# Reading the moving operand, and writing the sums, from the last token to the first

## The chip, the cores and the metric

The kernel runs on one core of a Trainium2 chip. The metric is the device time of one execution in microseconds, as the median of several runs. All times below are of this one core.

## What is computed

A two-layer decoder trunk over 256 tokens of width 1024, with a memory of 256 rows. Cut to what matters:

```python
def reference(x, mem, positions, ...):
    h = x
    for layer in range(2):
        hn = rmsnorm(h, norm_mix_g[layer])
        h = h + (sb_moba_mixer if layer == 0 else fox_mixer)(hn, ...)     # q/k/v (and gate) projections, 16 heads, output projection
        h = h + memory_cross_attention(rmsnorm(h, norm_xa_g[layer]), rmsnorm(mem, norm_mem_g[layer]), ...)
        h = h + conv_ffn(rmsnorm(h, norm_ffn_g[layer]), ...)              # up 1024 -> 2 x 2816, causal conv of width 3, silu(gate) * val, down
    return rmsnorm(h, final_norm_g)
```

Most of the arithmetic lies in products of weights with activations: the projections of the mixers, those of the cross-attention and the two of the MLP.

## The kernel before

Activations are held transposed: 128 features on the partitions, 256 tokens along the row, eight such tiles for the width of 1024. A product therefore has the weights as the stationary operand (128 x 128) and a tile of tokens as the moving one (128 x 256), and its sums lie in PSUM as 128 features by 256 tokens.

Precision is kept by splitting. Each weight block comes in as f32 (`raw`, loaded by SP's queue), ScalarE rounds it to the reduced type float32r (`whi`, line 126) and VectorE subtracts to get the rest (`wlo`, line 127). Activations are split likewise into a high and a low tile. A product of the two is then three products on TensorE: high by high, weight-high by activation-low, weight-low by activation-high. `proj` (lines 262 to 272) writes them, all on line 268, and every product on that line loads its own 128 x 128 weights. For a width of 1024 that makes 24 products into one PSUM tile; the down-projection has 66, in three weight blocks.

The names in the profile are those of the tiles. Moving tiles of line 268: `xh`/`xl` (the normed residual; 8 pairs), `gh`/`gl` (head outputs, the normed memory, and the MLP's gated values; 16 pairs), `part` (the first six of the MLP's gated pairs), `xn` (the renormalised input of the up-projection, 8 pairs from line 755 on). Sums: `acc` (two PSUM banks) and `sc` (four). The pools `xin`, `qkv` and `parts` that hold the moving tiles, and `wsp` that holds `whi` and `wlo`, lie in SBUF with gaps of 64, 256 and 64 bytes set by `shift`.

`proj_nat` (line 282) is the other form of product, with the activations as the stationary operand and the weights moving; it makes the values of the attentions and isn't touched. Attention scores, transposes (line 414, 697, 840), rope's product with a constant rotation (line 474, in f32), and the sums of squares for the norms (line 241, one moving column) aren't touched either.

The order on TensorE is the order in which the code is written (a manual schedule for that engine); the other engines are ordered by the tile scheduler. In the mixers attention steps are interleaved with the projections by `Pipe`; in the MLP of each layer 44 up-projections of 24 products follow one another, then 8 down-projections of 66.

The consumers of the sums read a whole PSUM tile once its last product is done: `evac_row` and `residual` (line 519) on VectorE, `glu` on ScalarE and VectorE, in ascending order of tokens.

Of the kernel before, what the change touches and what calls it, by code (L numbers as in the profile page):

```python
# [69 lines left out]
def trunk(ctx: ExitStack, tc: tile.TileContext, a: dict, out: bass.AP):  # L70
    nc = tc.nc
# [72 lines left out]
    for k in range(KD // 2):  # L144
        s = slice(k * 2 * P, (k + 1) * 2 * P)
# [116 lines left out]
    def proj(b, off, xs, ps, first=True, last=True, m=P, hooks={}):  # L262
        n = 0
        for k, (xh, xl) in enumerate(xs):
            s = slice(off + k * m, off + k * m + m)
            end = last and k == len(xs) - 1
            for w, x in ((b.hi, xh), (b.hi, xl), (b.lo, xh)):
                nc.tensor.matmul(ps[:m], w[:, s], x, start=first and n == 0, stop=end and w is b.lo)  # L268
                n += 1
                if n in hooks:  # L270
                    hooks[n]()
        return ps
# [268 lines left out]
    def mixer(layer, st):  # L541
# [47 lines left out]
        for g in range(4):  # L589
            def pair(i, hooks=({}, {})):  # L590
                wi = w[6 * g + 4 * i:6 * g + 4 * i + 2]
                q = proj(block(wi[0]), 0, xs, accA(), hooks=hooks[0])
                if hooks[0]:
                    return q, lambda: proj(block(wi[1]), 0, xs, accA(), hooks=hooks[1])
                q = evac_row(q, st, "q", 3, True)
                pipe.tick()
                k = evac_row(proj(block(wi[1]), 0, xs, accA()), st, "k", 3, False)
                pipe.tick()
                return q, k
# [344 lines left out]
```

## Time and profile before

| | |
|---|---|
| median of 3 runs | 716.21 us (714.2 to 717.5) |
| profiled execution | 717.27 us |
| its span, first to last instruction | 715.5 us |
| mean granted TensorE clock | 0.991 |
| TensorE busy | 695.3 us (97%), 5,751 products |
| weight loads busy (overlap TensorE) | 666.2 us (93%), 5,751 |
| VectorE, ScalarE, GpSimd busy | 575.1, 467.6, 74.2 us |
| HBM read | 114.25 MB, 161 GB/s over the span |

Engines in the rows: PE is TensorE's products, PEld its weight loads, DVE is VectorE, ACT ScalarE, POOL GpSimd. A row of a group gives line, engine, operation, output<-inputs by tile name, shape, count, busy time in us and the mean of one in ns. The time of one product in the rows (some 0.28 us) is from its start to the modelled end of its sums; products overlap, so the pace is read from start to start. In a row that merges several instructions, the time runs from the first's start to the last's end.

### The profile page before, as it was taken

How to read it: one execution, taken by the hardware profiler on the slowest of the kernel's cores; microseconds unless marked ns; L12 is line 12 of the kernel's file. 1: busy time of each engine (PE TensorE's matmuls, PEld its weight loads, DVE VectorE, ACT ScalarE, POOL GpSimd, SP SyncE). 2: the span in 40 equal slices, each digit the busy share in tenths (PEclk: the TensorE clock that was granted, in tenths of full speed). 3: DMA queues.
4: the chain of work that ended last, by engine and by line, in shares of the span. 5: the costliest groups of instructions: out<-in, count | busy, mean ns of one | idle time of the engine just before them, and what ended most of it. 6: DMA issues, size and time to landing. Idle time of an engine off the chain costs nothing. (4 is left out here: it accounts for less than half of the span.)

```text
span 715.5 us, 15077 instructions
## 1 busy us (share of the span) xinstructions
PE 695.3 (97%) x5751; PEld 666.2 (93%) x5751; DVE 575.1 (80%) x1195; ACT 467.6 (65%) x942; POOL 74.2 (10%) x82
## 2 busy tenths in 40 slices
PE   8989999999999999999999999999999999999995
PEld 5979998988999999999999889898899999999995
DVE  6997698687999988856669989958889998886541
ACT  6876866577787766644466868746778776664431
POOL 1200020212400000001200000012150000000110
PEclk9989999999999999999999999999999999999998
DMA  8745432343565655565651743515346566656601
GB/s 299 284 145 180 148 119 89 93 148 113 207 189 196 209 195 175 170 186 167 214 164 33 265 125 112 177 56 182 119 177 178 196 210 193 186 164 189 184 6 59
DMA packets 34968, 116.32 MB, mean 163 GB/s; under 512 B 4080, under 2 KB 6224, under 8 KB 34896
## 3 DMA queue, kind: packets, MB, share of 16 engines
q1 hardware_dynamic: 34896, 115.36, 50.8%
q8 instruction: 45, 0.74, 0.4%
q14 instruction: 27, 0.22, 0.1%
HBM read 114.25 MB, written 1.05 MB: 161 GB/s over the span
## 5 line engine op out<-in xcount | busy, mean ns | idle before, releaser
L126 ACT ACTIVATE whi<-raw 128x512 fp32r<-128x512 f32 (+2 forms) x296 | 231.0, 807 | 129.3 <-PE acc L268 80.8
L127 DVE TENSOR_TENSOR wlo<-raw,whi 128x512 fp32r<-128x512 f32 (+2 forms) x296 | 269.1, 925 | 56.4 <-ACT whi L126 54.1
L268 PE MATMUL sc<-xn,whi 128*128 128x256 f32 x768 | 136.9, 281 | 0.0
L268 PEld LDWEIGHTS sc<-xn,whi 128*128 128x128 f32 x768 | 117.9, 189 | 0.0
L268 PE MATMUL acc<-gh,whi 128*128 128x256 f32 x400 | 113.3, 283 | 0.2
L268 PE MATMUL acc<-gl,whi 128*128 128x256 f32 x400 | 111.5, 279 | 0.1
L268 PE MATMUL acc<-gh,wlo 128*128 128x256 f32 x400 | 111.2, 278 | 0.0
L268 PE MATMUL sc<-xn,wlo 128*128 128x256 f32 x384 | 107.9, 281 | 0.0
L268 PE MATMUL acc<-xh,whi 128*128 128x256 f32 x336 | 98.6, 293 | 2.4 <-DVE h L519 0.9
L268 PE MATMUL acc<-xh,wlo 128*128 128x256 f32 x336 | 94.4, 281 | 2.5 <-DVE wlo L127 2.5
L268 PE MATMUL acc<-xl,whi 128*128 128x256 f32 x336 | 95.4, 284 | 0.7 <-DVE xl L175 0.6
L226 POOL TENSOR_TENSOR sq<-sq 128x256 f32<-128x256 f32 x42 | 41.3, 984 | 508.6 <-ACT sq L220 467.6
L268 PEld LDWEIGHTS acc<-gh,whi 128*128 128x128 f32 x400 | 75.5, 189 | 2.3 <-ACT gh L170 0.9
L268 PEld LDWEIGHTS acc<-gl,whi 128*128 128x128 f32 x400 | 75.1, 188 | 0.3 <-DVE gl L171 0.3
L268 PEld LDWEIGHTS acc<-gh,wlo 128*128 128x128 f32 x400 | 75.4, 188 | 0.0
L268 PEld LDWEIGHTS sc<-xn,wlo 128*128 128x128 f32 x384 | 72.9, 190 | 0.0
L268 PEld LDWEIGHTS acc<-xh,whi 128*128 128x128 f32 x336 | 64.0, 190 | 7.0 <-issue 2.5
L268 PE MATMUL acc<-xn,whi 128*128 128x256 f32 x384 | 68.9, 281 | 0.0
L268 PEld LDWEIGHTS acc<-xh,wlo 128*128 128x128 f32 x336 | 63.8, 190 | 2.9 <-DVE wlo L127 2.9
L268 PEld LDWEIGHTS acc<-xl,whi 128*128 128x128 f32 x336 | 63.8, 190 | 2.5 <-DVE xl L175 1.9
L268 PEld LDWEIGHTS acc<-xn,whi 128*128 128x128 f32 x384 | 58.9, 189 | 0.0
L268 PE MATMUL acc<-xn,wlo 128*128 128x256 f32 x192 | 54.0, 281 | 0.0
(218 smaller groups left out, 1402.5 us busy)
## 6 DMA issues: line engine op xcount, KB each, us to landing
raw<-up SPq DMA_DIRECT2D x88, 512.0 KB
raw<-down SPq DMA_DIRECT2D x32, 448.0 KB
raw<-fox_in SPq DMA_DIRECT2D x24, 512.0 KB
raw<-ab_in SPq DMA_DIRECT2D x23, 512.0 KB
raw<-down SPq DMA_DIRECT2D x16, 512.0 KB
raw<-ab_out SPq DMA_DIRECT2D x8, 512.0 KB
raw<-fox_out SPq DMA_DIRECT2D x8, 512.0 KB
raw<-xa_k SPq DMA_DIRECT2D x4, 512.0 KB
```

Source lines behind the costliest of these rows:

```text
L126: i = nc.scalar.activation(hi[:, s], raw[:, s], AF.Copy)
L127: j = nc.vector.tensor_sub(lo[:, s], raw[:, s], hi[:, s].bitcast(F32))
L226: nc.gpsimd.tensor_tensor(sq, sq, self.acc, op=ALU.add)
L268: nc.tensor.matmul(ps[:m], w[:, s], x, start=first and n == 0, stop=end and w is b.lo)
```

## The change

On line 268 both the moving operand and the output get a reversed free axis. The weights stay as they are. The instruction then carries a step of -1 element and the address of the last column as its start, for the moving tile and for the PSUM tile alike, so column j of the moving tile still gives column j of the sums. This holds for all 4,632 products of `proj`, the 16-row forget-gate product among them. The order of instructions on every engine is the same as before, and so are all SBUF and PSUM addresses of tiles.

```diff
             for w, x in ((b.hi, xh), (b.hi, xl), (b.lo, xh)):
-                nc.tensor.matmul(ps[:m], w[:, s], x, start=first and n == 0, stop=end and w is b.lo)
+                nc.tensor.matmul(ps[:m][:, ::-1], w[:, s], x[:, ::-1], start=first and n == 0, stop=end and w is b.lo)
                 n += 1
```

## Prediction

> **What bounds the kernel now.** I read the page first: the share of each engine, the clock, the chain that ended last. The rows are the page's.
>
> ```profile
> span 715.5 us, 15077 instructions
> ...
> PE 695.3 (97%) x5751; PEld 666.2 (93%) x5751; DVE 575.1 (80%) x1195; ACT 467.6 (65%) x942; POOL 74.2 (10%) x82
> ...
> PEclk9989999999999999999999999999999999999998
> ...
> PE acc L268 14%; PE sc L268 11%; PE acc L282 0%; POOL sq L226 0%; DVE wlo L127 0%; DVE mx L685 0%; PE sc L697 0%; ACT sq L220 0%; PE sc L840 0%; PE misc L256 0%; DVE part L313 0%; DVE xl L175 0%; PE po L732 0%; ACT xh L174 0%; DVE h L519 0%
> ```
>
> TensorE is busy for 97% of the span at nearly the full clock, and the chain that ended last is almost wholly line 268, the line that the change edits. Next, the stretches view: line 268 alone over the whole span (TensorE busy, and the count in brackets), then four stages with all engines.
>
> ```profile
> 0.00:715.50 715.50, 562.17 (x4632) 0.99 0.51 163
> ```
>
> ```profile
> core 0: us, PE busy (x) PEld busy (x) DVE busy (x) ACT busy (x) POOL busy (x), PEclk, DMA share, GB/s
> ...
> 200.00:300.00 100.00, 100.00 (x851) 100.00 (x851) 92.86 (x162) 69.31 (x116) 0.00 (x0) 1.00 0.60 191
> 300.00:360.00 60.00, 60.00 (x522) 60.00 (x522) 36.83 (x47) 28.44 (x43) 7.68 (x7) 1.00 0.63 185
> ...
> 540.00:640.00 100.00, 100.00 (x852) 100.00 (x851) 93.40 (x163) 70.51 (x117) 0.00 (x0) 1.00 0.61 191
> 640.00:700.00 60.00, 60.00 (x517) 60.00 (x516) 33.37 (x45) 24.85 (x33) 6.48 (x6) 1.00 0.42 122
> ```
>
> 4,632 products are edited. In the four MLP stretches TensorE never rests, and the pace is 320 us / (851 + 522 + 852 + 517) = 116.7 ns a product. So the question of this change is one number: the time from one product's start to the next's. Every nanosecond of it is worth 4.6 us over the kernel, less what the waits between stages give back. TensorE's largest wait on another engine is small, so little can be given back:
>
> ```profile
> PE acc L268 <- DVE wlo L127: 2.5, 2, 1.8
> ```
>
> What sets the pace? In the timeline of TensorE (start, then time in us, products merged per row) I take three stretches that differ in the moving tile.
>
> ```profile
> 364.74 0.28 PE L268 MATMUL acc<-xl,whi 128*128 128x256 f32 x1
> ...
> 365.87 0.28 PE L268 MATMUL acc<-xh,wlo 128*128 128x256 f32 x1
> ```
>
> ```profile
> 254.82 0.28 PE L268 MATMUL acc<-xn,wlo 128*128 128x256 f32 x1
> ...
> 256.00 0.40 PE L268 MATMUL sc<-xn,whi 128*128 128x256 f32 x2
> ```
>
> ```profile
> 300.77 0.28 PE L268 MATMUL acc<-part,wlo 128*128 128x256 f32 x1
> ...
> 301.61 0.40 PE L268 MATMUL acc<-part,whi 128*128 128x256 f32 x2
> ```
>
> Between the first and last row lie 10, 10 and 7 starts: 1.13 / 10 = 113 ns, 1.18 / 10 = 118 ns, 0.84 / 7 = 120 ns. Same shape, same line, same clock, three paces. They aren't tied to a tile for good, as the chain shows in layer 1's down-projection (66 products in 7.80 and in 7.65 us, so 118.2 and 115.9 ns) and in its up-projection (48 in 5.65 us, 117.7 ns):
>
> ```profile
> 530.50 5.65 PE sc L268 x48
> ...
> 654.25 7.80 PE acc L268 x66
> ...
> 662.27 7.65 PE acc L268 x66
> ```
>
> The weight loads sit beside the products. The first two rows are loads in the 113 ns stretch; the third, at the kernel's end, is loads for products that stream a single column.
>
> ```profile
> 364.86 0.19 PEld L268 LDWEIGHTS acc<-xh,whi 128*128 128x128 f32 x1
> 364.97 0.19 PEld L268 LDWEIGHTS acc<-xl,whi 128*128 128x128 f32 x1
> ...
> ```
>
> ```profile
> 707.88 0.74 PEld L241 LDWEIGHTS misc<-const,sq 128*128 128x128 f32 x6 [0.99 <-ACT sq L220]
> ```
>
> Six loads in 0.74 us, one of them 0.19 long: (0.74 - 0.19) / 5 = 110 ns each, though there is next to nothing to stream. So loading 128 weight columns costs 110 ns by itself, and each product of line 268 needs a fresh load: the loop of load and start is a floor near 113 ns whatever the 256 moving columns do, and those columns must fit in it already, since 113 ns is reached.
>
> **The change part by part.** Nothing is added, removed or moved: the same 4,632 instructions in the same order, with the same weights and waits. Two address patterns of each run backwards, the moving tile's 256 columns in SBUF and the 256 sums in PSUM. Both are turned alike, so every sum lands where it did, and all 24 (or 42, or 66) products of one accumulation go the same way. Whoever reads a PSUM tile waits for the last product of it as before, and each product's 256 columns are complete at the same moment; no reader can start earlier or later for the direction. SBUF traffic, DMA and the other engines are untouched. So the sum has one term, 4,632 times the change of the pace, and no row of this trace shows a backward pattern on TensorE. I bound it.
>
> From below: the pace can't fall under the load's loop, 113 ns. All 4,632 from 116.7 to 113 would be 17 us less. The likelier partial gain is that the products on xn, which run at 117.7 to 118 now, drop to 113. Their counts:
>
> ```profile
> L268 PE MATMUL sc<-xn,whi 128*128 128x256 f32 x768 | 136.9, 281 | 0.0
> L268 PE MATMUL sc<-xn,wlo 128*128 128x256 f32 x384 | 107.9, 281 | 0.0
> L268 PE MATMUL acc<-xn,whi 128*128 128x256 f32 x384 | 68.9, 281 | 0.0
> ...
> L268 PE MATMUL acc<-xn,wlo 128*128 128x256 f32 x192 | 54.0, 281 | 0.0
> ```
>
> That is 1,728 x 4.7 = 8 us. VectorE would still follow: it is busy 92.86 of 100 us there, and that stage would shrink to 113 / 117.7 x 100 = 96 us.
>
> From above there are two bounds. If backward reads keep every address clash and add some, the nearest row is the part tiles' 120 ns: 4,632 x 3.3 = 15 us more. And if TensorE can't take two neighbouring columns together when they descend, the nearest row is an f32 product of the same width, rope's line 474, which issues one product on q and one on k; each shows as two records:
>
> ```profile
> 87.70 0.59 PE L474 MATMUL misc<-q,const 128*128 128x256 f32 x2
> 88.14 0.59 PE L474 MATMUL misc<-k,const 128*128 128x256 f32 x2
> ```
>
> 0.44 us for two records, 220 ns each, against 117 ns: a pass of 256 columns at about half the rate. That would be 4,632 x 103 = 477 us more.
>
> I take zero. The stream has to fit under a 110 ns load, so a start-up cost of a few nanoseconds is covered by the load, and a descending walk touches the same addresses as an ascending one, neighbour after neighbour. That cover is gone as soon as the stream itself takes longer than the load's loop; then all of the excess is paid, because TensorE has no idle time.
>
> The Trainium skill speaks to the paces: TensorE: Matmul & The Clock Gate, section "Step-by-step: what each phase is for", says that the moving operand and the weight load have a read port of SBUF each, so that loading the next weights takes nothing from the running product. By that rule the direction of one stream could not matter to the other, and the sum would be zero with no gain or loss of the 113-to-120 kind. The trace doesn't bear it out fully: 113, 118 and 120 ns at one shape and one clock say that operands' places or the two streams' phase matter.
>
> **The rivals.** Forecast A, the pace stays as it is, stage by stage: 717.3 us for the profiled execution, 1.1 us above the median of the three runs, so 716 as the median, 712 to 720 with the spread of the runs (714.2 to 717.5).
>
> B, faster: running the other way, the moving reads meet the weight reads at other moments, and more of the kernel runs at 113 ns. For it: the three paces above, with 118 held through the whole of both up-projections. Against it: one and the same tile kind (the down-projection's) shows 118.2 and 115.9 ns in alternate column blocks, so the pace also hangs on how a stretch began, and that the change leaves alone. From 716 - 17 = 699 to about 712; the xn products alone give 708.
>
> C, slightly slower: the same mechanism with the other sign. All at 118 is 4,632 x 1.3 = 6 us more, 722; all at 120 is 731. For it: nothing held the reversed phase at 113, and only a part of the kernel is at 113 now, which can be lost. Against it: the floor and the ceiling are both near, so most of the kernel can only lose 2 ns.
>
> D, much slower: descending columns are taken one at a time, by SBUF's reads or by PSUM's writes, and the stream replaces the load as the bound. It decides as soon as the stream passes some 113 ns a product. 716 + 477 = 1,193 us, with TensorE busy throughout and all other engines waiting for it. For it: line 474 shows that this array does walk 256 columns at 220 ns in one mode, so the full rate isn't given for every kind of operand. Against it: neighbours stay neighbours; only their order turns.
>
> The Trainium skill has a rule that would bring D about. Advanced Engine Details and Errata, section "PSUM Cachelines", says "Any non-contiguous AP significantly slows down matmuls". It goes on that every two consecutive elements should be contiguous, in lines of 8 bytes, that is two f32 sums; columns 255 and 254 share such a line, and by that sentence nothing would be lost. No run shown here has a backward or stepped PSUM write of TensorE, so the trace decides neither reading.
>
> That the change doesn't do what it says is A again: if the turned patterns were brought back into ascending order on the way to the chip, the time is 716.
>
> **How the numbers follow.** A 0.37, B 0.26, C 0.20, D 0.17. A is the likeliest, so 716. The range leaves out D, far off and with 0.17 of the chance, and spans B to C: 699 to 731, rounded in to 700 and out to 732; A's own is 712 to 720. Half a per cent, about what a measurement of this kernel can tell from no change, is 3.6 us. A spills 0.02 to each side; B counts as faster (0.28 in all), C and D as slower (0.39), which leaves 0.33.
>
> **What would show it.** In the profile after, one figure decides: the starts of line 268's products in the timeline of the same stretches. A: 118 ns on xn, 120 on part, 113 or 118 on xh and gh, and 48 of them in 5.65 us in the chain. B: 113 on xn, and the up-projection's 48 in 5.4 us. C: the 113 ns stretches gone, or paces over 118. D: some 215 to 220 ns everywhere, PEld's rows with gaps of 0.1 us, VectorE's share of the span near 50% instead of 80%. If only one of the two patterns costs something, the profile after can't say which; a kernel with one of them turned would. The forecast is wrong if line 268's mean pace in the 200 to 300 us stretch moves by over 1 ns.

## The result and the profile after

| | before | after |
|---|---|---|
| median of 8 runs each | 715.21 us (710.04 to 719.13) | 721.82 us (718.89 to 723.39) |
| ratio, 95% interval | | 1.0113 (1.0077 to 1.0149) |
| span of the profiled execution | 715.5 us | 721.6 us |
| mean granted clock in it | 0.991 | 0.986 |

The change costs 1.1%, which is rival C of the prediction and not the forecast. The page after, the same three lines:

```profile
span 721.6 us, 15078 instructions
...
PE 702.9 (97%) x5751; PEld 673.9 (93%) x5751; DVE 575.2 (80%) x1195; ACT 467.8 (65%) x942; POOL 73.9 (10%) x82
...
PEclk7989999999999999999999999999999999999999
```

TensorE is busy for the same share and the other engines for the same time, so no engine has become a new bound. In the stretches view, the four MLP stages (columns as before):

```profile
200.00:300.00 100.00, 100.00 (x851) 100.00 (x851) 93.30 (x163) 70.41 (x117) 0.00 (x0) 1.00 0.61 191
300.00:360.00 60.00, 60.00 (x509) 60.00 (x509) 37.17 (x48) 29.11 (x44) 6.66 (x6) 1.00 0.61 182
...
540.00:640.00 100.00, 100.00 (x851) 100.00 (x850) 93.99 (x163) 71.62 (x119) 1.95 (x3) 1.00 0.59 187
640.00:700.00 60.00, 60.00 (x511) 60.00 (x510) 36.23 (x50) 27.14 (x38) 6.39 (x5) 1.00 0.47 137
```

The up-projections, on xn, are as they were: 851 and 851 products in 100 us against 851 and 852. The stretches of the down-projections are slower: 509 products in 60 us against 522 (117.9 ns against 114.9), and 511 against 517 (117.4 against 116.1). TensorE's timeline shows which pace has gone. In this place before, on the gh tiles, nine starts took 1.02 us, 113 ns each:

```profile
310.64 0.28 PE L268 MATMUL acc<-gh,whi 128*128 128x256 f32 x1
...
311.66 0.28 PE L268 MATMUL acc<-gh,whi 128*128 128x256 f32 x1
```

After, nine starts on the gh tiles take 1.06 us, 118 ns each:

```profile
309.74 0.28 PE L268 MATMUL acc<-gh,whi 128*128 128x256 f32 x1
...
310.80 0.28 PE L268 MATMUL acc<-gh,whi 128*128 128x256 f32 x1
```

The chain says the same of layer 1, whose column blocks took 7.80 and 7.65 us in turn and now take 7.81 each:

```profile
535.95 5.65 PE sc L268 x48
...
659.90 7.81 PE acc L268 x66
667.92 7.81 PE acc L268 x66
```

Counted over all products of line 268 that follow one another within 135 ns (4,472 before, 4,458 after), the mean from start to start is 116.7 ns before and 118.0 after. Before, 1,232 of them came after 113 or 114 ns; after, one did. The products come in the same order in both, so each of these times can be set beside its own in the other profile. The fast ones of before take 5.6 us more in sum, all the others together 0.04 us more: within the pace, the loss is the fast pace and nothing else.

The spans differ by 6.1 us, and that this is so near 5.6 us is partly chance. The first 20 us hold 20 products fewer after than before, which put the changed kernel 2.5 us behind; the granted clock in them was 0.74 in place of 1.00 (before, then after):

```profile
0.00:20.00 20.00, 16.86 (x86) 12.24 (x87) 12.69 (x31) 11.67 (x25) 3.07 (x8) 1.00 0.87 310
```

```profile
0.00:20.00 20.00, 16.73 (x66) 12.00 (x67) 10.81 (x24) 11.53 (x23) 2.23 (x8) 0.74 0.86 310
```

In the rest, shorter gaps on line 268 and on the other lines gave back 2.0 us, nearly all of it in the mixers and the cross-attentions.

### The profile page after: what moved, and what is told of

It reads as the page before. It is cut to its first block, busy times and chain, and to the rows that moved or that the text cites. A ratio compares the mean times of both kernels' runs of the same rounds, so it can differ in the third digit from the quotient of the medians.

```text
span 721.6 us, 15078 instructions
## 1 busy us (share of the span) xinstructions
PE 702.9 (97%) x5751; PEld 673.9 (93%) x5751; DVE 575.2 (80%) x1195; ACT 467.8 (65%) x942; POOL 73.9 (10%) x82
## 5 line engine op out<-in xcount | busy, mean ns | idle before, releaser
L268 PE MATMUL acc<-gh,wlo 128*128 128x256 f32 x400 | 112.7, 282 | 0.0
L268 PE MATMUL acc<-xh,whi 128*128 128x256 f32 x336 | 100.2, 298 | 2.5 <-ACT xh L174 1.5
L268 PE MATMUL acc<-xh,wlo 128*128 128x256 f32 x336 | 96.2, 286 | 2.0 <-DVE wlo L127 2.0
L268 PE MATMUL acc<-xl,whi 128*128 128x256 f32 x336 | 97.2, 289 | 0.4
```

The source lines that it names most:

```text
L268: nc.tensor.matmul(ps[:m][:, ::-1], w[:, s], x[:, ::-1], start=first and n == 0, stop=end and w is b.lo)
```

## Experiments: which of the two patterns

**Only the reads reversed.**

```diff
-                nc.tensor.matmul(ps[:m][:, ::-1], w[:, s], x[:, ::-1], ...
+                nc.tensor.matmul(ps[:m], w[:, s], x[:, ::-1], ...
```

> Only the moving operand is reversed; the sums are written first token to last, so their tokens come out in reverse order and the output is not the reference's. Reading theory (the slowdown comes from the order in which the moving columns are fetched from SBUF while the next weights are fetched): as the changed kernel, ratio to before 1.008 to 1.015, no stretch at 113 ns a product, and a period of three in the up-projection near 120, 115, 118 ns. Writing rival (descending PSUM writes cost the time): as before, within 0.4% of it, with 113 ns stretches in the first mixer and 117 to 118 ns in the up-projection. Chance rival (which of two paces a stretch falls into is a matter of how it began, and the profiled runs only differed in that): both paces again in some mixture, ratio 0.995 to 1.01.

Measured: 721.05 us, ratio 1.007 (1.0041 to 1.0099), just under the expected 1.008. In its stretches view and its chain:

```profile
300.00:360.00 60.00, 60.00 (x509) 1.00 0.59 183
...
640.00:700.00 60.00, 60.00 (x511) 1.00 0.44 132
```

```profile
657.77 7.81 PE acc L268 x66
```

The counts, 509 and 511, and the 7.81 us are those of the changed kernel; in the up-projection the starts go 120, 115, 118 ns round and round, as they do there.

**Only the writes reversed.**

```diff
-                nc.tensor.matmul(ps[:m][:, ::-1], w[:, s], x[:, ::-1], ...
+                nc.tensor.matmul(ps[:m][:, ::-1], w[:, s], x, ...
```

> Only the output is reversed; the moving operand is read first token to last, so the tokens of the sums come out in reverse order and the output is not the reference's. Reading theory: as before, ratio 0.996 to 1.004, 113 ns stretches there. Writing rival: as the changed kernel, ratio 1.008 to 1.015, no 113 ns stretch, period of three near 120, 115, 118 ns. Chance rival: both paces in some mixture, ratio 0.995 to 1.01.

Measured: 718.25 us, ratio 1.0008 (0.9967 to 1.0050).

```profile
300.00:360.00 60.00, 60.00 (x521) 1.00 0.60 185
```

```profile
656.11 7.80 PE acc L268 x66
664.13 7.65 PE acc L268 x66
```

521 products and the turns of 7.80 and 7.65 us: the kernel before. So the reads carry the loss and the writes carry nothing that can be measured. The reading theory held in both, by the traces more clearly than by the times: 1,568 starts came after 113 or 114 ns with the writes reversed, none with the reads reversed. That 1,568 is more than the 1,232 of the kernel before, which suggests that the share of the fast pace changes from one execution to the next; with one trace of each kernel this is not shown.

## Experiments: the pace by itself

**A bench of line 268's products alone.** The rest of the kernel is left out; the loop, run twice for a group of 48 products, is

```python
for k in range(8):
    ...
    for wi, xi in ((0, 0), (0, 1), (1, 0)):      # hi*hi, hi*lo, lo*hi
        m = x[xi][:, off + k * T:off + (k + 1) * T]
        nc.tensor.matmul(acc[:, ::-1] if write else acc, w[wi][:, s], m[:, ::-1] if read else m, ...)
```

> Leaves out the whole network: 64 groups of 48 products in the same pattern (weight-high by high, weight-high by low, weight-low by high), each with its own weight load, with nothing else running, at eight distances in SBUF between moving tile and weights (64 bytes apart, letters A to H), each in four ways: both ascending (up), both descending (down), only the reads descending (read), only the writes descending (write), and all that twice with two lengths of pause ahead of a group. Reading theory: write equals up and read equals down at every distance, within 0.5 ns a product; up shows 113 ns at some distances or some of its groups, down and read never below 117. Writing rival: read equals up, and write equals down. Chance rival: 113 and 118 ns come up in all four ways, without regard to direction. If the distance sets the pace, up differs between letters by up to 7 ns (113 to 120) and repeats between its two passes; if only the beginning sets it, the two passes differ.

Distance is the moving tile's address in SBUF less that of the weights, modulo 256 bytes. In its chain each group is a row: start, time of 48 products, the way and the letter. Letters A to D stand for 0, 64, 128 and 192 bytes; E to H, 256 bytes on, repeat them. From a group's first start to its second some 220 ns pass, and the last product adds its 0.28 us; from the ninth start on, 6.03 us stands for 120.0 ns a product, 5.96 for 118.4, 5.93 for 117.8 and 5.74 for 113.3. In the second pass that first time is some 190 ns in half of the groups, so that 5.91 there is 117.8 ns too. These paces are means: 117.8 is 117 to 119 ns from start to start ascending, and 115 to 120 in turn descending.

```profile
22.63 5.96 PE downA L101 x48
...
42.09 5.93 PE upB L101 x48
48.53 6.03 PE downB L101 x48
...
94.07 5.74 PE upD L101 x48
100.31 5.94 PE downD L101 x48
106.75 5.93 PE readD L101 x48
113.19 5.74 PE writeD L101 x48
...
222.76 6.03 PE upA L101 x48
...
306.68 5.91 PE upD L101 x48
```

With the core otherwise idle the same paces come up, so they need neither DMA nor the other engines. Reversed reads alone equal the full reversal at every letter in both passes. Reversed writes alone equal none (D) in the first pass; in the second, writeD stays at 113.3 ns while upD is at 117.8, and at F it is the other way round, against the expected half nanosecond: these are the two distances, 192 and 64 bytes, at which ascending reads showed both paces. The distance bears on which paces a direction can have, and at 0 bytes descending is the faster of the two (5.96 against 6.03 us). At 192 bytes, where the kernel before has 4,326 of its 4,632 products, ascending has two paces, 113.3 and 117.8 ns, on the same addresses (upD in both passes): distance and direction don't settle which, and a group keeps the one it has. Descending has only 117.8 there. The two theories of the expectation both hold a part: distance and direction limit the paces, and where there are two, something in how the group began must choose.

**Finer steps.** The same bench, ascending and descending only, at steps of 16 bytes.

> Leaves out the whole network, as the run before: groups of 48 products alone on the core, here at sixteen distances between moving tile and weights, 16 bytes apart (letters A to P, 0 to 240 bytes), ascending (up) and descending (down), in three passes with pauses of different length ahead of a group. Distance theory (a product's pace is set by direction and by the distance modulo 256 bytes): A, E, I, M repeat the four coarse paces, up 120.0, 117.8 or 113.3, 118.7, 113.3 or 117.8 and down 118.4, 120.0, 120.0, 117.8 ns; a letter that has one pace has it in all three passes; 113.3 in up only, at E, M and perhaps beside them. If the fast pace belongs to the ascending direction as such, no down group is under 116 ns at any distance. If it belongs to particular distances of either direction, which the coarse steps of 64 bytes happened to miss for down, some down groups between the coarse letters show 113.3 as well. Rival (the beginning alone decides): each letter shows 113 and 118 in the three passes without a rule.

Here E is 64 bytes and H 112:

```profile
93.57 5.93 PE upE L101 x48
100.00 6.03 PE downE L101 x48
...
132.51 5.77 PE upH L101 x48
138.78 6.04 PE downH L101 x48
...
209.93 6.00 PE upN L101 x48
...
530.95 5.70 PE upE L101 x48
```

The 16 descending letters gave 117.8 to 120.1 ns in all their groups; no distance has a fast pace for them here. A letter doesn't always keep one pace: descending at 80 bytes gave 120.0 ns in two passes and 117.8 in the third, ascending at 160 bytes 117.4, 120.0 and 118.7. Ascending had 113.3 in some pass at 16, 64, 112 and 192 bytes, and at 112 in all three (113.3 to 113.8).

## Experiments: the prices carried back into the kernel

**Four placements that move the weights.** A gap of 256 bytes in place of 64 ahead of the weights, and the first gap moved ahead of the part tiles, puts the distances at 0; the weights' own tiles made 256 bytes longer and used from byte 16 on, with one gap of 128 bytes in place of the three and one buffer fewer for the attention's exponentials, puts them at 112. Each was built ascending and descending.

The weights' high tile at 112:

```diff
-        hi = wsp.tile([P, BLK], F32R, tag="whi", name="whi")
+        hi = wsp.tile([P, BLK + 64], F32R, tag="whi", name="whi")[:, 4:4 + BLK]
...
```

> The kernel before (ascending) with moving tiles and weights 0 bytes apart modulo 256. Distance theory: 120.0 ns a product, no stretch at 113, ratio 1.016 to 1.025. Direction-alone rival: as before, ratio 0.995 to 1.005.

> The changed kernel (descending) with the distance of 0. Distance theory: 118.4 ns a product, 4,600 x 1.7 ns = 8 us more than before, ratio 1.007 to 1.015, and so about 1% faster than the ascending kernel at this distance: the same edit with the other sign. Direction-alone rival: descending is slower than ascending here too, by about 1%.

> The kernel before (ascending), with moving tiles and weights placed 112 bytes apart modulo 256 instead of 192 (128 for the part tiles), and one exponent buffer fewer to make room. Distance theory: 113.3 to 113.8 ns a product nearly everywhere, 4,600 x 3.1 ns = 14 us less than before, ratio 0.977 to 0.985, and the up-projection's 48 products in 5.45 us in place of 5.65. Direction-alone rival (ascending has some mixture of 113 and 118 wherever the tiles lie): ratio 0.995 to 1.005. Third possibility: VectorE, busy 93 of 100 us in the up-projection before, becomes the bound, TensorE waits for the weights' low part, and the ratio stays over 0.99.

> The changed kernel (reads and writes descending) at the same distance of 112 bytes. Distance theory: 120.0 ns a product, 4,600 x 3.3 ns = 15 us more than before, ratio 1.016 to 1.025, so that the same edit costs some 4% at this placement. Direction-alone rival: as the changed kernel, ratio 1.007 to 1.015.

Measured at 0: ascending 726.58 us, ratio 1.0154 (1.0115 to 1.0194), just under the expected 1.016; descending 723.10 us, 1.0090 (1.0057 to 1.0124). The up-projection's 48 products in the chains, ascending and then descending:

```profile
544.06 5.76 PE sc L268 x48
```

```profile
542.77 5.68 PE sc L268 x48
```

5.76 / 48 = 120.0 and 5.68 / 48 = 118.3 ns, as the bench had it, and the edit under study makes this kernel faster, by 1.0090 / 1.0154, 0.6% in place of the 1% expected. The two intervals overlap by a little, but each of the eight descending runs (720.03 to 725.09 us) is faster than each of the six ascending ones (725.87 to 729.44). Direction as such is not what costs.

Measured at 112: ascending 726.38 us, ratio 1.0138 (1.0099 to 1.0176); descending 720.73 us, 1.0071 (1.0045 to 1.0097). Ascending, then descending:

```profile
547.00 5.76 PE sc L268 x48
```

```profile
549.13 5.65 PE sc L268 x48
```

The distance theory fell here: it asked for 113.3 and 120.0 ns, and the kernels show 120.0 and 117.7, with the edit saving 0.7% (1.0071 / 1.0138). VectorE isn't the reason, since TensorE was busy for all of the 100 us in both up-projection stretches of both kernels. One thing differs from the bench: there the moving tile was displaced from a multiple of 64 bytes, here the weights were.

**Displacing the moving tile instead.** All moving tiles but xn become slices of one tile named xs, from byte 48 on; rope's and the forget gates' scratch moves elsewhere. The control has the same instructions with xs from byte 0 on (`[0]` in place of `[12]`, and 192 bytes for the first gap) and the distances at 192. Line 274 is line 268 of the kernel before.

```diff
+    ring = pool("ring").tile([P, 60 * T + 16], F32R, name="xs")
+    at, used, free = {}, {}, [12]
...
+        return ring[:, o:o + T]
```

> Ascending. The moving tiles of the normed residual, the head outputs and the MLP's gated values (2,886 of line 268's products, now all slices of one tile named xs) start 48 bytes past a multiple of 64, the weights stay on one, so that the distance is 112 bytes with the moving tile displaced, as in the bench, and not the weights, as in the run at 112 bytes that missed. The xn tiles (1,728 products) stay at 192. Two-places theory (the moving tile's own place within 64 bytes counts beside the distance): 113.3 to 113.8 ns on xs in place of 115.7 and on the former part tiles of 119, 118 on xn, 7 us less than before, ratio 0.986 to 0.995, and 1% less than the next run, its control. If displaced tiles are slower in the full kernel however they are displaced: 119 to 120 ns on xs and a ratio over 1.01.

> Ascending. The same program as the run before, instruction for instruction, with the xs tiles on a multiple of 64 and every distance at 192 bytes. The control for the rearrangement: both paces, 113.3 and 117.8 ns, as in the kernel before (ratio 0.995 to 1.005, somewhat below 1 if the former part tiles, at 128 before, gain 2 to 5 ns on 288 products).

> Descending reads and writes on the placement of the first of these three runs. The bench had 120.0 ns for descending at 112 bytes and 117.8 at 192. Two-places theory: 120.0 ns on xs, 118 on xn, 2,886 x 6.5 ns = 19 us more than the ascending kernel at the same placement, ratio to before 1.012 to 1.021. Rival (the direction costs the same 1.1% at every placement): 1.0% over the ascending one.

Measured: 711.84 us, ratio 0.9930 (0.9897 to 0.9963); control 712.75, 0.9937 (0.9904 to 0.9969); descending 724.05, 1.0104 (1.0071 to 1.0137). The chains of the three over layer 1's down-projection, where the moving tiles are all xs:

```profile
646.84 7.54 PE acc L274 x66
654.38 0.22 PE sc L847 x2
654.60 7.54 PE acc L274 x66
```

```profile
649.98 7.78 PE acc L274 x66
...
665.97 7.52 PE acc L274 x66
```

```profile
660.07 7.91 PE acc L274 x66
...
668.20 7.92 PE acc L274 x66
```

114.2 ns every time, 114 or 118 in the control, 119.9 descending: near the bench's 113.3 to 113.8 and 120.0 ns at 112 bytes, and its 113.3 or 117.8 at 192. At this placement the edit costs (1.0104 / 0.9930) 1.8%, and not the rival's 1.0%, though descending lies just under its expected 1.012. The two ascending kernels do not differ as wholes, against the expectation of 1%, and the control lies just under its expected 0.995. In the traces xs did gain: 114.3 ns over all its products against 116.2 in the control, some 5 us, with profiled spans of 706.8 and 710.8 us. The stretches of the xn products, which have the same 192 bytes in both (the first, then the control), show what else moves the total:

```profile
200.00:300.00 100.00, 99.96 (x880) 99.71 (x879) 95.23 (x165) 71.46 (x119) 0.30 (x1) 1.00 0.61 197
540.00:640.00 100.00, 99.96 (x850) 99.99 (x850) 92.54 (x159) 69.65 (x117) 0.00 (x0) 1.00 0.60 192
```

```profile
200.00:300.00 100.00, 100.00 (x854) 99.75 (x854) 93.50 (x163) 69.80 (x117) 0.30 (x1) 1.00 0.60 192
540.00:640.00 100.00, 100.00 (x881) 99.76 (x881) 95.76 (x169) 73.08 (x121) 0.00 (x0) 1.00 0.60 197
```

In each kernel one up-projection fell into the fast pace (880 or 881 products in 100 us, 113.5 ns) and one did not, where the kernel before had both slow. Only one execution of each kernel has a trace, so what xs gained and what this draw gives can't be told apart by the medians. Both kernels beat the two of this study, by 0.6 to 0.7% of the one before. In the control's trace that is the draw: its xn products took 115.1 ns in the mean against 117.8 before, 1,728 x 2.7 = 4.7 us, as much as its span is shorter (715.5 and 710.8). The former part tiles, 128 bytes off before, gain in both as well (in layer 1 from 119.3 to 115.6 ns in the control and 113.6 at 112 bytes), but they are only 288 products, 1 to 2 us.

**Both places at once.** The last bench, with the weights displaced from a multiple of 64 by 0 to 48 bytes (A to D) and the moving tile by as much more.

> Leaves out the whole network, as the two benches before it. Groups of 48 products at three distances between moving tile and weights (nil 0, mid 112, far 192 bytes), ascending (up) and descending (down), with the weights displaced by 0, 16, 32 or 48 bytes from a multiple of 64 (letters A to D) and the moving tile displaced by as much more, so that the distance is kept; two passes. Distance theory: the four letters are alike, 48 products in 6.03 us at nil, 5.74 at mid and 5.74 or 5.93 at far for up, 5.96, 6.03 and 5.93 for down. Two-places theory (the place of the weights within 64 bytes counts as well, which would explain why the run at 112 bytes with displaced weights missed): A as just said, but upmidB, where the weights are displaced by 16 bytes as in that run, near 6.0 us in place of 5.74, and downmidB below upmidB.

```profile
55.09 5.77 PE upmidA L101 x48
61.36 6.04 PE downmidA L101 x48
67.90 5.74 PE upfarA L101 x48
...
93.58 5.96 PE upmidB L101 x48
100.04 5.94 PE downmidB L101 x48
106.48 5.74 PE upfarB L101 x48
```

At 112 bytes, moving the pair by 16 bytes turns 5.77 into 5.96 us ascending and 6.04 into 5.94 descending; C is like A, and D near B (118.3 to 120.0 ns ascending, 117.8 descending, over both passes). That is what the kernels with displaced weights showed, so the distance isn't enough: the weights' own place, here an even or odd multiple of 16 bytes, counts beside it. At 192 bytes all four letters keep 113.3 ascending.

Could it be the moving tile's place alone, whatever the weights' is? Two comparisons of these runs say no. The moving tile 208 bytes past a multiple of 256 gave 119.0, 119.1 and 116.7 ns with the weights on such a multiple (the three passes of upN), and 113.3 in both passes with the weights 16 bytes on (upfarB). And the ascending kernel at 0 bytes has its xn tiles where the kernel before has them; of the two operands only the weights have moved, by 192 bytes, and xn went from 117.8 to 120.0 ns. The paces belong to the pair.

## Why the prediction was wrong, point by point

- **What bounds the kernel** held: the time from product to product cost 5.6 us, and the profiled spans differ by 6.1 us. The waits did give a little back, as the prediction allowed, 2.0 us. The first 20 us, with their lower granted clock, took 2.5 us more, which no term stands for and which looks like a draw of the execution: over the other runs the mean granted clock went from 0.981 to 0.997 for the kernel before and from 0.986 to 0.997 for the changed one.
- **The step that failed** is "I take zero", the value of the one term of the sum, with its reason that a descending walk touches the same addresses as an ascending one and that a small cost is covered by the load. The term measured 1.3 ns a product. The runs show that the order of the reads, together with the places of moving tile and weights, limits which paces come up: 113.3 or 117.8 ns ascending at this kernel's 192 bytes, only 117.8 descending. The load covered nothing of that: the fast pace of 113.3 ns was already close to the 110 ns that the prediction read for a load. The three paces quoted in the prediction were the evidence for it and were taken for scatter that the change leaves alone.
- **The last sign** of the prediction, a mean pace that moves by over 1 ns in the 200 to 300 us stretch, did not come (851 products before and after), though the forecast fell. That stretch had no fast pace to lose. The sign named for C did come: "the 113 ns stretches gone".
- **The bounds** held: no descending kernel went below 113 or above some 120 ns. The range of 700 to 732 held the time; it was the forecast of no change that fell. The 120 ns, read from seven starts on the part tiles, is 119.2 over all of theirs; as a ceiling it held, by the benches' 120.0.
- **Rival C** was the case, by its own first price: "All at 118 is 4,632 x 1.3 = 6 us more, 722". Its condition, "only a part of the kernel is at 113 now, which can be lost", is what happened. That the time met 722 to the microsecond is partly luck: in the profiled pair the 2.5 us of the first stretch and the 2.0 us given back nearly cancel.
- **Rival B** was right that the direction changes the pace, and had the sign wrong at this placement. At 0 bytes the sign is B's. Its reason, that the moving reads meet the weight reads at other moments, was not tested.
- **Rival D** is out: reversed writes cost 1.0008 (0.9967 to 1.0050) and reversed reads stay within 7 ns a product of the fastest pace, far from the 220 ns of line 474. Of the Trainium skill's rule in Advanced Engine Details and Errata, section "PSUM Cachelines", the sentence that two consecutive elements should be contiguous agrees with this; read strictly, as a price on any order but the ascending one, the other does not hold here.
- **The rule on ports** of the Trainium skill, in TensorE: Matmul & The Clock Gate, section "Step-by-step: what each phase is for", gave zero as well. The benches, alone on the core, show 113.3 to 120.1 ns at one shape by placement, direction and how a group began, and the pace belongs to the places of both operands. So by these runs the weight load and the moving reads are not independent, and the measurement decides.
- **What stays open** is the mechanism inside: that the two streams' reads meet in SBUF fits all runs but was only argued. No run reversed the order of the weights, or shows whether the load or the product is the one held up. What in a stretch's beginning picks the fast or the slow pace is open too: the benches only varied the pause ahead of a group, and no rule came out.

## What to carry to other kernels

Where a stream of products each loads its own weights, read the pace from start to start, stretch by stretch: several paces at one shape and one clock were here the sign that the operands' places count, and the edit of the address pattern then had a price that depends on them. Test such an edit at two placements before giving it a sign: here it is +1.1%, +1.8%, about -0.6% and about -0.7%. And a forecast of "no change" because the same work is done needs the floor to have slack; here the fast pace, 113.3 ns, was the lowest that any group of products showed.

## What was not expected of the hardware

A pace, once entered, can hold for hundreds of products: in the ascending kernel with xs at 112 bytes, some 670 products followed one another at 113.3 ns in one up-projection and some 820 at 117.8 in the other, at the same distance. The distance counts in steps as small as 16 bytes, and modulo 256 (in the first bench E to H repeat A to D, but for the two distances with two paces). And reversing the order of the PSUM writes has no price that could be measured: 1.0008 (0.9967 to 1.0050).
